# Shift and scale of the first layer loaded in pairs, its first projection begun between them, and a second mixer's adaLN as matmuls

## Chip, cores and metric

One core of one Trainium2 chip. The metric is the device time of the kernel in microseconds (us); the median of the runs is compared. Everything below is one launch on that core.

## What is computed

A decoder trunk of two layers on x (1 x 512 x 1024, float32) with a conditioning vector c (1 x 1024). Each layer has a token mixer (layer 0: native sparse attention, NSA; layer 1: HGRN2, a gated linear recurrence) and a mixture of 16 gated-MLP experts (MoE). Each of these four sub-layers takes a shift, a scale and a gate from c:

```python
cond = jax.nn.silu(c)
for layer in range(DEPTH):
    mod = jnp.einsum('bd,sde->sbe', cond, ada_w[layer]) + ada_b[layer][:, None, :]
    ...
    shift, scale, gate = jnp.split(mod[0], 3, axis=-1)
    h = rms_norm(x, norm_g[layer, 0]) * (1.0 + scale[:, None, :]) + shift[:, None, :]
    y = nsa_mixer(h, ...) if layer % N_MIXERS == 0 else hgrn2_mixer(h, ...)
    x = x + gate[:, None, :] * y
    shift, scale, gate = jnp.split(mod[1], 3, axis=-1)
    ...  # the same norm, then hier_moe, then the gated residual
```

Two pieces matter here. `cond @ ada_w` (adaLN) is one row of 1024 numbers times a 1024 x 3072 matrix for each of the four sub-layers. `h @ w_in` is the first thing that a mixer does with the normalized x; in the NSA mixer 512 of its columns are those of the compressed keys and values (called kv here).

## The kernel before, in words

**adaLN.** `ada_parts(l, s)` (L164) gives six parts for sub-layer s of layer l, 512 columns (2 MB of weights) each: t = 0, 1 are the halves of the shift, 2, 3 of the scale, 4, 5 of the gate. Each part is a load and a generator `part(t, w)`. Parts are counted through the program as 6 (2 l + s) + t; below `POOLED` = 16, `part` does 32 matmuls of TensorE (L185) with the conditioning column as the stationary side, eight at a time with a yield after each eight. Numbers 16 to 23, the gate of the second mixer and all of the second MoE, go another way: ACT scales the eight 128 x 512 blocks by their conditioning column (L192), POOL adds the blocks in three steps of 2048, 1024 and 512 columns (L198), and TensorE sums the partitions with four matmuls against ones (L202). Either way the row is copied by DVE (L209), transposed by TensorE (L211) and put into `mod` by DVE (L214, L217); a gate is added into `gg` (L206).

**The start.** SP's queue loads x, then the four adaLN parts of the first sub-layer in the order 0, 2, 1, 3, then the kv weights (`load_cols`, L435), all of them before any matmul. `norm_T` (L258) makes the normalized x and, block by block, transposes it (L275) and applies scale and shift: ACT writes the high part `hThi` (L280), DVE a copy `hf` (L281), and DVE or POOL the low part `hTlo` (L283). With `before`, the blocks of feature rows 0 to 511 (k = 0 to 3) come first, after parts 0, 2 and 1 and a small table (L456); those of rows 512 to 1023 come after part 3.

**The projections.** A float32 product is made of three matmuls: weights and h are each split into a high and a low part, and high x high, low x high and high x low are summed (L337 to L339). `split_k` (L306) splits one 128 x 512 block of weights: high on ACT (L310), low on DVE (L311). `proj_stream` (L317) goes over tiles of 512 columns; it asks for the next tile's weights ahead, and splits them between the matmuls of the tile's last piece. The first tile is kv: four pieces of 128 tokens, 8 x 3 matmuls each, 96 in all.

**The ring.** Weights of adaLN and of projections share `ring`, which has two slots of 2 MB (`RING`), and are loaded by SP's queue (some early ones of the HGRN stage by POOL's). A load waits until its slot's last reader is done, and what stands behind it on the queue waits too.

**The HGRN stage.** `merge(heads(), ada, HADA)` (L1026) weaves three things together: the eight heads' recurrence, the projection stream, and the adaLN parts 16 to 23, one at a time (`in_turn(..., 1)`), 0.45 steps of a part for each step of a head. A head's recurrence doubles its blocks level by level: TensorE makes the scores of a level (`lvA_ps` to `lvD_ps`, L1043 to L1073), DVE multiplies Q and K by decays for the next (L1080, L1081) and TensorE waits for these. The instructions are put into one order for each engine when the program is built. The output product of the mixer (L373 to L375) needs all of the heads' outputs and the last two ring slots, and the second MoE follows.

Of the kernel before, what the change touches and what calls it, by code (L numbers as in the profile page):

```python
# [32 lines left out]
POOLED = 16  # L33
ADDED = 1

PARTS = ((0, 1, 2), (3,))
# [26 lines left out]
def kernel(ctx: ExitStack, tc: tile.TileContext, I, out, dbg=None, upto="all"):  # L63
# [100 lines left out]
    def ada_parts(l, s):  # L164
# [16 lines left out]
        def part(t, w):  # L181
            if 6 * (2 * l + s) + t < POOLED:
                ps = mm_ps("ada_ps")
                for q in range(0, NK, 2):
                    side_by_side([lambda k=k, g=g: nc.tensor.matmul(  # L185
                        ps[32 * g:32 * g + 32, 0:128], cond[:, k:k + 1].to_broadcast([128, 32]),
                        w[:, k, 128 * g:128 * g + 128], start=(k == 0), stop=(k == NK - 1))
                        for k in (q, q + 1) for g in range(4)])
                    yield
            else:  # L190
                for k in range(NK):
                    nc.scalar.activation(w[:, k], w[:, k], AF.Copy, scale=cond[:, k:k + 1])  # L192
                    if k % 2:
                        yield
                n = NK
                while n > ADDED:
                    n //= 2
                    nc.gpsimd.tensor_tensor(w[:, 0:n], w[:, 0:n], w[:, n:2 * n], op=ALU.add)  # L198
                ps = mm_ps("ada_ps")
                for k in range(n):  # L200
                    for g in range(4):
                        nc.tensor.matmul(ps[32 * g:32 * g + 32, 0:128], onef.to_broadcast([128, 32]),  # L202
                                         w[:, k, 128 * g:128 * g + 128], start=(k == 0), stop=(k == n - 1))
                yield
            if t >= 4:
                nc.vector.tensor_add(gg[:, t - 4], gg[:, t - 4], ps[:, 0:128])  # L206
                return
            row = small.tile([128, 128], F32, tag="adarow", bufs=2, name="adarow")
            nc.vector.tensor_copy(row, ps[:, 0:128])  # L209
            tp = tp_ps("ada_tp")  # L210
            nc.tensor.transpose(tp[:, 0:128], row, ident)  # L211
            b0 = (2 * l + s) * 24 + 4 * t
            m4 = mod[:, 4 * t:4 * t + 4]
            nc.vector.tensor_add(m4, tp[:, 0:128:32], cols[:, b0:b0 + 4])  # L214
            if t >= 2:
                g0 = 96 + (2 * l + s) * 8 + 4 * (t - 2)
                nc.vector.scalar_tensor_tensor(m4, m4, 1.0, cols[:, g0:g0 + 4], op0=ALU.add, op1=ALU.mult)  # L217
# [40 lines left out]
    def norm_T(pool, work, mod, load, before=None):  # L258
# [9 lines left out]
        for i, (half, k) in enumerate(blocks):  # L268
            if before and i % 4 == 0:
                before(i // 4)  # L270
# [46 lines left out]
    def proj_stream(pool, h, tiles, ws=None, last=None):  # L317
# [10 lines left out]
        for n, (_, pieces) in enumerate(tiles):  # L328
            nxt = []
            w = tiles[n + 1][0]() if n + 1 < len(tiles) else None  # L330
            for p, (kind, i, done) in enumerate(pieces):
                c = slice(128 * i, 128 * i + 128)
                ps = mm_ps("pr_ps")
                for k in range(NK):
                    a, b = ws[k]
                    if kind == "tok":
                        nc.tensor.matmul(ps, hi[:, k, c], a, start=(k == 0), stop=False)  # L337
                        nc.tensor.matmul(ps, hi[:, k, c], b, start=False, stop=False)  # L338
                        nc.tensor.matmul(ps, lo[:, k, c], a, start=False, stop=(k == NK - 1))  # L339
                    else:  # L340
                        nc.tensor.matmul(ps, a[:, c], hi[:, k], start=(k == 0), stop=False)
                        nc.tensor.matmul(ps, b[:, c], hi[:, k], start=False, stop=False)
                        nc.tensor.matmul(ps, a[:, c], lo[:, k], start=False, stop=(k == NK - 1))
                    if w is not None and p == len(pieces) - 1:
                        nxt.append(split_k(pool, w, k))
                    if k % 2 and k < NK - 1:
                        yield
# [75 lines left out]
    def nsa_heads(l, load, win, m, st, ada0, fill):  # L423
# [6 lines left out]

        def load_cols(c0, step, n):
# [9 lines left out]
        with sb("first") as wk, sb("adaw", bufs=2) as aw:  # L441
            ada0 = [ada0[i] for i in (0, 2, 1, 3)]
            xs = {t: load(wk, t) for t in range(NT)}
            early = [ada0[i][0](p) for i, p in enumerate((ring, aw, aw, ring))]
# [14 lines left out]

            def before(q):  # L460
# [7 lines left out]
            wkvc = []  # L468
            h = norm_T(pool, wk, mods[l, 0], lambda work, t: xs[t], before)
            ws0 = [split_k(wsp, wkvc[0], k) for k in range(NK)]  # L470
# [174 lines left out]
        for half in range(2):  # L645
            with sb("qkv") as qp:
# [3 lines left out]
                with sb("proj") as wk:  # L650
                    if half == 0:
                        with sb("cmp") as cp:
# [3 lines left out]
                                                      for t in range(NT)])] + half_tiles(0, qkv, wk), ws0, last)  # L656
# [18 lines left out]
                            for _ in range(16):  # L675
                                next(s)
# [1090 lines left out]
```

## Time and profile before

| what | value |
| --- | --- |
| runs | median 1475.61 us of 3 (1474.67 to 1477.06) |
| profiled execution | 1478.35 us, its span 1476.5 us |
| mean granted TensorE clock of the span | 0.944 |
| busy: PE, DVE, ACT, POOL | 87%, 49%, 32%, 15% of the span |
| start, until the kv product ends | about 66.8 us |
| HGRN stage, until the second MoE's router | about 850 to 1114 us |

Shares of the span are means over stages with different limits: the rows further below are taken stage by stage. PE is the matmul side of TensorE, PEld its loading of weights, SPq, ACTq and POOLq are queues in which an engine issues loads. A row's "[3.22 <-DVE K L1081]" says that the engine stood idle for 3.22 us before it and that DVE's write of K at line 1081 released it. "PEclk" is the TensorE clock that was granted, as a share of full speed.

### The profile page before, as it was taken

To read this page: it belongs to the slowest core of one execution; us is meant where nothing else is said; L and a number is where in the kernel's file an instruction comes from. 1 tells how busy PE (TensorE), PEld (TensorE's weight loads), DVE (VectorE), ACT (ScalarE), POOL (GpSimd) and SP (SyncE) were. 2 spreads that over 40 slices of the span, in tenths; PEclk is the share of its full clock that TensorE was granted. 3 is DMA by queue.
4 is the path that set the end of the run, shared out by engine and by line. 5 is a ranking of instruction groups with operands and counts; after the bars stand their busy time and mean duration, and the time that the engine had idled before them with its cause. 6 is when DMAs were issued, how large, how long until landed. Compare 5 with 4: busy or idle time off the path is not lost. (4 is left out here: it accounts for less than half of the span.)

```text
span 1476.5 us, 25266 instructions
## 1 busy us (share of the span) xinstructions
PE 1291.1 (87%) x10122; PEld 767.6 (52%) x10123; DVE 723.1 (49%) x1791; ACT 468.1 (32%) x1071; POOL 225.5 (15%) x198
## 2 busy tenths in 40 slices
PE   4998899988989699999983998888979699999983
PEld 3776555765558333333323866566767543333330
DVE  2636886468854722222217476777665641222213
ACT  2523555336533211111115434344533121111110
POOL 1202212222100100000014025222130100000002
PEclk9999999999999799999996999999989799999997
DMA  9702552634564899999986222433338699999995
GB/s 354 206 11 85 176 185 91 252 121 152 192 265 157 282 368 343 376 381 334 384 325 182 86 103 87 157 115 115 115 115 299 235 343 365 360 377 335 367 397 193
DMA packets 168733, 346.42 MB, mean 235 GB/s; under 512 B 17236, under 2 KB 40620, under 8 KB 168605
## 3 DMA queue, kind: packets, MB, share of 16 engines
q1 hardware_dynamic: 135984, 276.80, 52.6%
q0 software_dynamic: 10560, 38.54, 8.0%
q10 hardware_dynamic: 22060, 29.34, 6.0%
q8 instruction: 84, 1.38, 0.4%
q14 instruction: 45, 0.36, 0.1%
HBM read 320.73 MB, written 23.93 MB: 233 GB/s over the span
## 5 line engine op out<-in xcount | busy, mean ns | idle before, releaser
L1452 PE MATMUL h_ps<-w,hgt 128*32 128x256 f32 (+1 forms) x2240 | 332.9, 488 | 0.0
L1452 PEld LDWEIGHTS h_ps<-w,hgt 128*32 128x32 f32 (+1 forms) x2240 | 111.8, 123 | 203.1 <-issue 172.4
L1479 PE MATMUL y_ps<-w,gT 128*32 128x256 f32 (+1 forms) x1120 | 163.6, 499 | 2.5 <-ACT gT L1468 2.1
L1458 DVE TENSOR_TENSOR g<-h_ps,g 32x256 f32<-32x256 f32 (+1 forms) x70 | 38.9, 556 | 253.7 <-ACT g L1456 253.1
L1456 ACT ACTIVATE g<-h_ps 64x512 f32<-64x512 f32 (+1 forms) x52 | 26.8, 516 | 368.2 <-PE h_ps L1452 346.2
L337 PE MATMUL pr_ps<-whi,hThi 128*128 128x512 f32 x288 | 119.6, 417 | 1.8 <-DVE qn L498 1.8
L338 PE MATMUL pr_ps<-wlo,hThi 128*128 128x512 f32 x288 | 115.6, 401 | 0.3 <-DVE wlo L311 0.3
L339 PE MATMUL pr_ps<-whi,hTlo 128*128 128x512 f32 x288 | 115.7, 402 | 0.2 <-DVE hTlo L283 0.2
L1479 PEld LDWEIGHTS y_ps<-w,gT 128*32 128x32 f32 (+1 forms) x1120 | 54.9, 125 | 97.3 <-issue 81.3
L1482 DVE TENSOR_TENSOR y<-y_ps,gate 128x512 f32<-128x512 f32 (+1 forms) x52 | 31.1, 598 | 123.3 <-PE y_ps L1479 107.5
L311 DVE TENSOR_TENSOR wlo<-w,whi 128x512 fp32r<-128x512 f32 x120 | 79.7, 702 | 23.0 <-ACT whi L310 22.8
L310 ACT ACTIVATE whi<-w 128x512 fp32r<-128x512 f32 x120 | 70.8, 629 | 39.0 <-SPq L1589 14.2
L782 ACT ACTIVATE P<-P,nm 128x128 f32<-128x128 f32 (+3 forms) x128 | 70.9, 556 | 36.9 <-DVE nm L780 35.8
L1416 POOL DMA_INDIRECT hg<-xnd,gidxp x26 | 23.7, 913 | 384.8 <-PE hg_tp L1428 383.0
L776 PE MATMUL s_ps<-kT,qT 128*128 128x256 f32 (+3 forms) x256 | 64.8, 358 | 12.0 <-DVE qn L498 6.9
L198 POOL TENSOR_TENSOR w<-w 128x2048 f32<-128x2048 f32 (+2 forms) x24 | 67.0, 2792 | 47.3 <-ACT w L192 46.1
L780 DVE CUSTOM_DVE_ANT_0 P<-s_ps,tb 128x128 f32<-128x128 f32 (+3 forms) x128 | 59.5, 485 | 21.5 <-PE s_ps L776 18.8
L1436 DVE TENSOR_SCALAR hgt<-hg_tp,mod 128x96 f32<-128x96 f32 (+2 forms) x128 | 43.7, 365 | 41.9 <-PE hg_tp L1428 36.4
L337 PEld LDWEIGHTS pr_ps<-whi,hThi 128*128 128x128 f32 x288 | 55.6, 193 | 15.1 <-issue 3.3
L339 PEld LDWEIGHTS pr_ps<-whi,hTlo 128*128 128x128 f32 x288 | 55.4, 192 | 12.2 <-DVE hTlo L283 0.4
L338 PEld LDWEIGHTS pr_ps<-wlo,hThi 128*128 128x128 f32 x288 | 55.9, 194 | 11.0 <-DVE wlo L311 0.7
L821 PE MATMUL p_tp<-ident,P 128*128 128x128 f32 x320 | 52.8, 282 | 8.2 <-DVE P L796 7.9
(361 smaller groups left out, 2121.9 us busy)
## 6 DMA issues: line engine op xcount, KB each, us to landing
w<-in_moe_w_dram SPq DMA_DIRECT2D x120, 1024.0 KB, 9.7
w<-in_moe_w_dram SPq DMA_DIRECT2D x32, 2048.0 KB, 9.5
w<-in_ada_w_dram SPq DMA_DIRECT2D x22, 2048.0 KB, 9.3
w<-in_hgrn_w_in_dram SPq DMA_DIRECT2D x12, 1024.0 KB, 6.9
tb<-tabd ACTq DMA_DIRECT2D x16, 456.0 KB, 3.8
yd<-y ACTq DMA_DIRECT2D x56, 128.0 KB, 5.0
w<-in_nsa_w_in_dram SPq DMA_DIRECT2D x3, 2048.0 KB, 8.1
yd<-zero POOLq DMA_DIRECT2D x12, 512.0 KB, 9.6
```

The costliest lines, as they stand in the source:

```text
L198: nc.gpsimd.tensor_tensor(w[:, 0:n], w[:, 0:n], w[:, n:2 * n], op=ALU.add)
L310: nc.scalar.activation(a, w[:, k], AF.Copy)
L311: nc.vector.tensor_sub(b, w[:, k], a.bitcast(F32))
L337: nc.tensor.matmul(ps, hi[:, k, c], a, start=(k == 0), stop=False)
L338: nc.tensor.matmul(ps, hi[:, k, c], b, start=False, stop=False)
L339: nc.tensor.matmul(ps, lo[:, k, c], a, start=False, stop=(k == NK - 1))
L776: nc.tensor.matmul(sp[:, :n], qT[:, (hd + j) % 8, 128 * t:128 * t + 128], kT[:, v, br, gl, :n], start=(v == 0), stop=(v == 1))
L780: nc.vector.tensor_tensor_reduce(ps, sp[:, :n], tbs[hd + j][:, 384 - 128 * t:512], scale=-1.0, scalar=3.0e38, op0=ALU.add, op1=ALU.min, ac ...
L782: nc.scalar.activation(ps, ps, AF.Exp, bias=nm[:, i:i + 1], scale=-1.0, accum_out=z[:, i:i + 1])
L821: nc.tensor.transpose(tp[:, 128 * (t - kc):128 * (t - kc) + 128], Ps[j][:, offs[t] + 128 * kc:offs[t] + 128 * kc + 128], ident)
L1452: nc.tensor.matmul(ps[m * j:m * j + m, :w], hgt[:, k, r:r + m], ws[half][:, x + i, c:c + w], start=(k == 0), stop=(k == NK - 1))
L1479: nc.tensor.matmul(ps[m * j:m * j + m, :w], gT[:, f, r:r + m], w2v[:, f, w * j:w * j + w], start=(f == 0), stop=(f == 3))
```

## The change

Two edits. First, at the start, the kv weights come as two loads of 1 MB (rows 0 to 511 and 512 to 1023), each behind one pair of adaLN parts (0, 2 and 1, 3); the kv product's first half (k = 0 to 3 of all four token pieces, 48 of 96 matmuls) is done as soon as the norm's first half is there, with part 1 after two pieces, part 3 after four and then the table; `proj_stream` goes on with k = 4 to 7 in the four sums already begun. Second, `part` has only the matmul way: parts 16 to 23 lose their ACT and POOL instructions and have 32 matmuls instead of four.

```diff
-POOLED = 16
-ADDED = 1
-
-PARTS = ((0, 1, 2), (3,))
...
         def part(t, w):
-            if 6 * (2 * l + s) + t < POOLED:
-                ps = mm_ps("ada_ps")
-                for q in range(0, NK, 2):
-                    side_by_side([...])
-                    yield
-            else:
-                for k in range(NK):
-                    nc.scalar.activation(w[:, k], w[:, k], AF.Copy, scale=cond[:, k:k + 1])
-                    if k % 2:
-                        yield
-                n = NK
-                while n > ADDED:
-                    n //= 2
-                    nc.gpsimd.tensor_tensor(w[:, 0:n], w[:, 0:n], w[:, n:2 * n], op=ALU.add)
-                ...
+            ps = mm_ps("ada_ps")
+            for q in range(0, NK, 2):
+                side_by_side([lambda k=k, g=g: nc.tensor.matmul(
+                    ps[32 * g:32 * g + 32, 0:128], cond[:, k:k + 1].to_broadcast([128, 32]),
+                    w[:, k, 128 * g:128 * g + 128], start=(k == 0), stop=(k == NK - 1))
+                    for k in (q, q + 1) for g in range(4)])
                 yield
...
+            if behind and n % 4 == 3:
+                behind(n // 4, (hi, lo))
...
-    def proj_stream(pool, h, tiles, ws=None, last=None):
+    def proj_stream(pool, h, tiles, ws=None, last=None, begun=()):
...
-                ps = mm_ps("pr_ps")
-                for k in range(NK):
+                early = n == 0 and p < len(begun)
+                ps = begun[p] if early else mm_ps("pr_ps")
+                for k in range(4 if early else 0, NK):
...
-            early = [ada0[i][0](p) for i, p in enumerate((ring, aw, aw, ring))]
+            early = []
+            for i, p in enumerate((ring, aw, aw, ring)):
+                early.append(ada0[i][0](p))
+                if i == 1:
+                    wkv = ring.tile([128, 8, 512], F32, tag="w", name="w")
+                if i % 2:
+                    load_rows(wkv, 1024, 2 * i - 2)
...
+            def behind(q, h):
+
+                for k in range(4 * q, 4 * q + 4):
+                    ws0.append(split_k(wsp, wkv, k))
                 if q == 0:
-                    wkvc.append(load_cols(1024, 512, 512))
-                for i in PARTS[q]:
-                    run(ada0[i][1](early[i]))
-                    if i == 2:
-                        table()
...
+                    for t in range(NT):
+                        begun.append(acc_ps("kv_ps") if t < 2 else mm_ps("kv_ps"))
+                        for k in range(4):
+                            tok_product(begun[t], h, ws0[k], t, k)
+                        if t % 2:
+                            run(ada0[2 + t // 2][1](early[2 + t // 2]))
+                    table()
```

In the changed file L181 stands for L185, L192 for L211, L256 for L275, L261 for L280, L293 for L310, L304 to L306 for L337 to L339, L331 to L333 for L341 to L343, and lines behind 600 are ten higher. The order of the attention and of both MoE stages is the same in both programs. It moves at these places.

On SP's queue at the start (x, adaLN weights, kv weights, constants), before:

```order
L1682 DMA xs<-in_x_dram 128x1024 x4
L91 DMA w<-in_ada_w_dram 128x8x512 x4
L435 DMA w<-in_nsa_w_in_dram 128x8x512
L474 DMA cst<-in_shape_consts_dram 128x396
L475 DMA trif<-in_shape_consts_dram 128x128
```

and with the change:

```order
L1692 DMA xs<-in_x_dram 128x1024 x4
L88 DMA w<-in_ada_w_dram 128x8x512 x2
L423 DMA w<-in_nsa_w_in_dram 128x4x512
L88 DMA w<-in_ada_w_dram 128x8x512 x2
L423 DMA w<-in_nsa_w_in_dram 128x4x512
L484 DMA cst<-in_shape_consts_dram 128x396
```

The first half of the kv weights has moved ahead of two adaLN parts; the bytes are the same.

On ACT at the end of the first norm (`hThi` is the norm's output, `whi` the high part of split weights; `w_192` of before is kv, `w_520` of before and `w_573` of the change the next tile), before:

```order
L310 ACTIVATE whi_467<-w_192 128x512
L280 ACTIVATE hThi_165<-h_tp_403,mod00_106 128x256
L280 ACTIVATE hThi_165<-h_tp_414,mod00_106 128x256
L280 ACTIVATE hThi_165<-h_tp_425,mod00_106 128x256
L310 ACTIVATE whi_471<-w_192 128x512
L310 ACTIVATE whi_475<-w_192 128x512
L280 ACTIVATE hThi_165<-h_tp_436,mod00_106 128x256
```

and with the change:

```order
L261 ACTIVATE hThi_168<-h_tp_472,mod00_106 128x256
L459 DMA tabd_134<-tabs_461 16x1040
L261 ACTIVATE hThi_168<-h_tp_472,mod00_106 128x256
L261 ACTIVATE hThi_168<-h_tp_483,mod00_106 128x256
L261 ACTIVATE hThi_168<-h_tp_494,mod00_106 128x256
L261 ACTIVATE hThi_168<-h_tp_483,mod00_106 128x256
L261 ACTIVATE hThi_168<-h_tp_505,mod00_106 128x256
L293 ACTIVATE whi_620<-w_573 128x512
L261 ACTIVATE hThi_168<-h_tp_494,mod00_106 128x256
L293 ACTIVATE whi_624<-w_573 128x512
L261 ACTIVATE hThi_168<-h_tp_505,mod00_106 128x256
```

The splits of kv have moved ahead of these rows, the table's store in among them, and two splits of the next tile stand ahead of the norm's last two activations (one row on the gate weights between them is left out).

On PE in the HGRN stage, around one adaLN part (`pr_ps` is the projection stream, `ho_ps` and `lvA_ps` the recurrence), before:

```order
L1124 MATMUL ho_ps<-vS,AD 128x128
L1124 MATMUL ho_ps<-vS,AO 128x128 x3
L1124 MATMUL ho_ps<-vS,AD 128x128
L202 MATMUL ada_ps<-w,onef 32x128 x4
L337 MATMUL pr_ps<-whi,hThi 128x512
L338 MATMUL pr_ps<-wlo,hThi 128x512
L339 MATMUL pr_ps<-whi,hTlo 128x512
```

and with the change:

```order
L332 MATMUL pr_ps<-hThi,wlo 128x512
L333 MATMUL pr_ps<-hTlo,whi 128x512
L1053 MATMUL lvA_ps<-Q,K 32x32 x16
L181 MATMUL ada_ps<-w,cond 32x128 x16
L304 MATMUL pr_ps<-whi,hThi 128x512
L305 MATMUL pr_ps<-wlo,hThi 128x512
L306 MATMUL pr_ps<-whi,hTlo 128x512
```

A part's matmuls, four in one place before, are 32 in up to four places, and they are now the first readers of the load. At the end of the stage the last adaLN part stood between the last head's levels, with `out_ps` behind it; now its last eight matmuls are ahead of the last head's levels and the first `out_ps` matmuls stand among the levels.

## Rows read from the trace of the kernel before

**Rows 1.** The page's first lines: the span, and each engine's busy us, share of the span and instructions.

```profile
span 1476.5 us, 25266 instructions
PE 1291.1 (87%) x10122; PEld 767.6 (52%) x10123; DVE 723.1 (49%) x1791; ACT 468.1 (32%) x1071; POOL 225.5 (15%) x198
```

**Rows 2.** Busy time in stretches of the start. Columns: stretch (us), its length, busy us (and instructions) of PE, PEld, DVE, ACT and POOL, granted clock, DMA share, GB/s.

```profile
33.00:47.43 14.43, 11.33 (x112) 8.97 (x109) 11.93 (x24) 10.71 (x22) 3.01 (x2) 0.88 1.02 226
47.43:66.80 19.37, 19.09 (x86) 15.26 (x84) 10.88 (x20) 8.65 (x15) 4.95 (x2) 1.00 0.72 207
66.80:110.50 43.70, 43.67 (x328) 30.59 (x327) 13.74 (x34) 9.02 (x22) 3.04 (x3) 1.00 0.14 49
```

**Rows 3.** PE in the order of time at the start (start, us, operation): the first adaLN part with the cause of the wait ahead, the fourth, and two kv matmuls.

```profile
15.40 3.64 PE L185 MATMUL ada_ps<-w,cond 128*32 128x128 f32 x64 [7.03 <-DMA w<-in_ada_w_dram]
...
34.85 1.95 PE L185 MATMUL ada_ps<-w,cond 128*32 128x128 f32 x64
...
45.44 0.39 PE L338 MATMUL pr_ps<-wlo,hThi 128*128 128x512 f32 x1
45.67 0.39 PE L339 MATMUL pr_ps<-whi,hTlo 128*128 128x512 f32 x1
```

**Rows 4.** ACT and its queue at the start, in the order of time: the table's store, the first split of the kv weights, a row of the norm.

```profile
33.88 2.28 ACTq L458 DMA_DIRECT2D tabd<-tabs  x1
...
39.81 1.15 ACT L310 ACTIVATE whi<-w 128x512 fp32r<-128x512 f32 x2
...
42.86 1.69 ACT L280 ACTIVATE hThi<-h_tp,mod 128x256 fp32r<-128x256 f32 x3
```

**Rows 5.** SP's queue at the start: the next tile's loads (four) and the one behind.

```profile
43.44 10.54 SPq L435 DMA_DIRECT2D w<-in_nsa_w_in_dram  x5
```

**Rows 6.** Busy time in the HGRN stage, from just ahead of the first part with POOL additions to the end of the projection stream's matmuls, and from there to the output product. Columns as in rows 2.

```profile
850.00:1080.36 230.36, 204.17 (x2303) 155.76 (x2302) 162.38 (x310) 98.51 (x190) 71.64 (x31) 0.94 0.33 111
1080.36:1098.29 17.93, 9.62 (x262) 7.83 (x261) 14.24 (x29) 5.49 (x12) 4.14 (x3) 0.75 0.60 218
```

**Rows 7.** Busy time in the seven stretches of that stage in which POOL adds (L198); the last of them, and the sum of all seven. Columns as in rows 2.

```profile
1066.56:1083.47 16.91, 15.65 (x134) 12.73 (x132) 3.15 (x5) 7.39 (x15) 16.59 (x6) 1.00 0.00 1
sum 68.21, PE 44.67 PEld 33.10 DVE 47.78 ACT 13.40 POOL 66.93; mean PE 6.38 PEld 4.73 DVE 6.83 ACT 1.91 POOL 9.56
```

**Rows 8.** The same for the eight stretches between them, from 850 to 1088 us: the sum.

```profile
sum 169.79, PE 164.68 PEld 127.06 DVE 119.69 ACT 86.37 POOL 7.77; mean PE 20.58 PEld 15.88 DVE 14.96 ACT 10.80 POOL 0.97
```

**Rows 9.** One of those stretches in the order of time, all engines.

```profile
1025.78 8.45 POOL L198 TENSOR_TENSOR w<-w 128x2048 f32<-128x2048 f32 x3 [7.74 <-ACT w L192]
...
1025.88 4.76 DVE L1081 TENSOR_TENSOR K<-K,Tc 128x256 f32<-128x256 f32 x1
...
1026.85 0.39 PE L342 MATMUL pr_ps<-hThi,wlo 128*128 128x512 f32 x1
...
1030.70 0.68 PE L1063 MATMUL lvC_ps<-Q,K 128*64 128x64 f32 x8 [3.22 <-DVE K L1081]
...
1032.00 0.63 PE L342 MATMUL pr_ps<-hThi,wlo 128*128 128x512 f32 x1
```

**Rows 10.** Another of them, in the order of time.

```profile
950.62 8.72 POOL L198 TENSOR_TENSOR w<-w 128x2048 f32<-128x2048 f32 x3
...
951.49 4.25 DVE L1138 TENSOR_TENSOR on<-on,gS 128x512 f32<-128x512 f32 x1
...
959.67 0.66 PE L1043 MATMUL lvB_ps<-Q,K 128*32 128x32 f32 x32 [6.17 <-DVE K L1081]
```

**Rows 11.** The instructions of three lines: duration in ns (least, median, most), first and last start in us, forms.

```profile
L198 POOL TENSOR_TENSOR w<-w x24: 1288/2415/4770, 862.9 to 1082.1; 128x2048 f32<-128x2048 f32 x8, 128x1024 f32<-128x1024 f32 x8, 128x512 f32<-128x512 f32 x8
...
L192 ACT ACTIVATE w<-w,cond x64: 705/712/727, 857.8 to 1072.0; 128x512 f32<-128x512 f32 x64
...
L1081 DVE TENSOR_TENSOR K<-K,Tc x56: 409/418/4759, 852.9 to 1097.5; 128x256 f32<-128x256 f32 x56
```

**Rows 12.** PE in the order of time: a quarter of an adaLN part as matmuls, during the attention, and the row behind it; then the four matmuls of a part in the HGRN stage, and the row behind them. A record of a matmul in a column group counts twice (x16 for eight, x8 for four).

```profile
388.16 0.64 PE L185 MATMUL ada_ps<-w,cond 128*32 128x128 f32 x16
388.73 0.44 PE L821 MATMUL p_tp<-ident,P 128*128 128x128 f32 x2
...
949.49 0.45 PE L202 MATMUL ada_ps<-w,onef 128*32 128x128 f32 x8
...
949.87 0.50 PE L341 MATMUL pr_ps<-hThi,whi 128*128 128x512 f32 x1
```

**Rows 13.** Loads of adaLN weights in the HGRN stage, by SP's queue and by POOL's: KB each, us from issue to landing.

```profile
w<-in_ada_w_dram SPq DMA_DIRECT2D x1, 2048.0 KB, 8.1
...
w<-in_ada_w_dram POOLq DMA_DIRECT2D x1, 2048.0 KB, 8.4
```

**Rows 14.** The end of the HGRN stage in the order of time: the last adaLN part's matmuls, the load of the output weights, their split, the first output matmul.

```profile
1085.99 0.66 PE L202 MATMUL ada_ps<-w,onef 128*32 128x128 f32 x16
1086.59 0.99 SPq L91 DMA_DIRECT2D w<-in_hgrn_w_out_dram  x2
...
1097.52 2.55 ACT L313 ACTIVATE whi<-w,gain 128x512 fp32r<-128x512 f32 x4
...
1098.29 0.79 PE L373 MATMUL out_ps<-whi,ohi 128*128 128x512 f32 x1 [1.34 <-ACT whi L313]
```

**Rows 15.** The second MoE. Columns as in rows 2.

```profile
1120.00:1450.00 330.00, 308.19 (x2124) 138.05 (x2124) 101.71 (x296) 62.24 (x132) 22.57 (x26) 0.96 0.94 338
```

More of the change, by code (lines that the diff above doesn't have):

```diff
@@ L256, in rms_rows, with norm_T @@
         return rs
-    def norm_T(pool, work, mod, load, before=None):
+    def norm_T(pool, work, mod, load, before=None, behind=None):
         hi = pool.tile([128, NK, T], F32R, name="hThi")
@@ L267, in norm_T @@
             blocks = [(half, k) for q in (0, 4) for half in range(2) for k in (q, q + 2)]
-        for i, (half, k) in enumerate(blocks):
-            if before and i % 4 == 0:
-                before(i // 4)
+        for n, (half, k) in enumerate(blocks):
+            if before and n % 4 == 0:
+                before(n // 4)
             c = slice(256 * half, 256 * half + 256)
@@ L315, in split_k, with tok_product @@
         return a, b
-    def proj_stream(pool, h, tiles, ws=None, last=None):
+    def tok_product(ps, h, ws, i, k):
+        hi, lo = h
+        a, b = ws
+        c = slice(128 * i, 128 * i + 128)
+        nc.tensor.matmul(ps, hi[:, k, c], a, start=(k == 0), stop=False)
+        nc.tensor.matmul(ps, hi[:, k, c], b, start=False, stop=False)
+        nc.tensor.matmul(ps, lo[:, k, c], a, start=False, stop=(k == NK - 1))
+    def proj_stream(pool, h, tiles, ws=None, last=None, begun=()):
         hi, lo = h
@@ L429, in nsa_heads, with load_rows @@
         tabd = dram.tile([HEADS, TBL], F32, name="tabd")
+        def load_rows(w, c0, k0):
+            loads.append(nc.sync.dma_start(out=w[:, k0:k0 + 4], in_=win[128 * k0:128 * k0 + 512, c0:c0 + 512]
+                                           .rearrange("(k p) n -> p k n", p=128)))
         def load_cols(c0, step, n):
@@ L458, in table @@
                 nc.scalar.dma_start(out=tabd, in_=tabs)
+            ws0, begun = [], []
             def before(q):
-                if q == 0:
-                    wkvc.append(load_cols(1024, 512, 512))
-                for i in PARTS[q]:
-                    run(ada0[i][1](early[i]))
-                    if i == 2:
-                        table()
-            wkvc = []
-            h = norm_T(pool, wk, mods[l, 0], lambda work, t: xs[t], before)
-            ws0 = [split_k(wsp, wkvc[0], k) for k in range(NK)]
+                for i in (0, 1) if q == 0 else ():
+                    run(ada0[i][1](early[i]))
+            def behind(q, h):
+                for k in range(4 * q, 4 * q + 4):
+                    ws0.append(split_k(wsp, wkv, k))
+                if q == 0:
+                    for t in range(NT):
[5 more added lines that the diff above has]
+                    table()
+            h = norm_T(pool, wk, mods[l, 0], lambda work, t: xs[t], before, behind)
             trif = wk.tile([128, 128], F32, name="trif")
@@ L655, in nsa_heads @@
                                                      [("tok", t, lambda ps, t=t: nc.scalar.activation(kv[:, t], ps, AF.Copy) and None)
-                                                      for t in range(NT)])] + half_tiles(0, qkv, wk), ws0, last)
+                                                      for t in range(NT)])] + half_tiles(0, qkv, wk), ws0, last, begun)
                             w1 = cp.tile([128, 2, 16, DH], F32, name="cw1")
@@ L674, in nsa_heads @@
                             nc.gpsimd.memset(x2[:, :, 0:4, 256:264], 0.0)
-                            for _ in range(16):
+                            for _ in range(8):
                                 next(s)
```

16 lines of the change are left out of this document (3 added, 13 removed).

## Prediction

> **What bounds the kernel now.** I first take each engine's share of the span: TensorE is busy for 87%, no other engine for half [rows 1]. That is a mean, so I then cut the span into stretches and look in each for time in which TensorE stands idle or runs at a lower clock. Only the start and the HGRN stage are edited. The stages behind them have their old order. The attention follows the start with TensorE gapless, 43.67 of 43.70 us [rows 2], and the second MoE is fed by loads, DMA share 0.94 [rows 15]. So what the start or the HGRN stage gives should move everything behind it and not be eaten.
>
> In the start, TensorE is busy in 11.33 of 14.43 us just before the kv product runs freely and then in 19.09 of 19.37 [rows 2]: almost all of the 96 kv matmuls stand behind the norm, while earlier TensorE waits for loads (7.03 us before the first part [rows 3]).
>
> The HGRN stage is the large case. From 850 to 1080.36 us TensorE is busy for 204.17 of 230.36, at a clock of 0.94: 26.2 us idle [rows 6]. The seven stretches in which POOL adds adaLN weights hold 68.21 us, and TensorE is busy in 44.67: 23.5 us idle in under a third of the time [rows 7]. The eight stretches between them hold 169.79 us with 164.68 busy: 5.1 idle [rows 8]. The order of time says how POOL does this. An addition starts at 1025.78, DVE's product for K starts 0.1 us later and takes 4.76 us, and TensorE stands for 3.22 us until K is written [rows 9]; the middle of that line's 56 is 418 ns [rows 11]. At 951.49 the same happens to another product with two SBUF operands (4.25 us), and a level's matmuls wait 6.17 us [rows 10]. Then the clock follows: a projection matmul takes 0.39 us before the wait and 0.63 after [rows 9].
>
> **The change, part by part.** The sum goes against the profiled execution, 1478.35 us with its span of 1476.5; that stands 2.74 above the median, 1475.61, and I subtract this at the end.
>
> *Price of the added matmuls.* A quarter of a part as matmuls starts at 388.16 and the next work at 388.73: 0.57 us, so 2.28 a part. The four matmuls against ones took from 949.49 to 949.87: 0.38 [rows 12]. Eight parts cost 8 x (2.28 - 0.38) = **+15.2 us** on TensorE. That is on the path: these matmuls fill no gap of their own, and I count all of it. A cold clock would make it more: the first part took 3.64 and the fourth 1.95 us [rows 3], so the ends are 8 x 1.57 = 12.6 and 8 x 3.26 = 26.1.
>
> *The removed work.* POOL loses 24 additions, all but a few of its 66.93 us in the seven stretches [rows 7], ACT 64 scalings of 0.71 us, 45 us [rows 11]. Neither engine is the bound, so this is worth only what waits for it: 23.5 us of idle time in the seven stretches, of which 16.91 - 15.65 = 1.3 lies in the last one, at the end of the stage [rows 7]. I take **-22.3** for 850 to 1080; 26.2 - 22.3 = 3.9 us of idle time stays. What stays is the levels' own chain, at 418 ns a product.
>
> *Clock.* 204.17 us at 0.94 is a loss of at most 204.17 x 0.06 = 12.2 us [rows 6]. The falls come behind the waits [rows 9], but the added matmuls and load waits can make new ones; between 0 and -12.2 I take **-8**.
>
> *New waits.* Before, ACT was the first reader of an adaLN load, with POOL and a part's yields behind it; now TensorE is, in order, with the projection and the levels queued behind. A load takes 8.1 us from issue to landing [rows 13], and its slot comes free when a tile's last block is split, by the order some 28 to 40 projection matmuls of 0.23 us [rows 3], 6 to 9 us, ahead of the part. So some of eight loads are late by 1 to 2 us. Nothing in the rows shows this wait. Its ends are 0 and 8 x 8.1 = 65 us (no overlap at all); it is nearest to the lower one, since all but two or three of the loads are issued a whole part ahead: **+2**. On the other side, the ring's projection weights no longer stand behind POOL's chain; I count nothing for that, as TensorE never waited for one there.
>
> *End of the stage.* Between the stream's last matmul and the output product TensorE is busy in 9.62 of 17.93 us [rows 6]. DVE starts there with K held up by the last addition, the last adaLN part's matmuls sit between the levels, and only behind them is the load of the output weights issued, at 1086.59; their split starts at 1097.52 and the first output matmul at 1098.29 [rows 14]. By the new order that slot is free before the last head's levels, and output matmuls stand among them. The ends are 0 (the levels' chain sets the end as before) and 8.3 (all of the idle time); I take the middle, **-4**.
>
> *Start.* 48 kv matmuls at 0.23 us [rows 3] are 11.0 us that could lie beside loads: one end is -11. The other end is +1: the norm's rows and the splits share ACT and DVE, which were busy for 10.71 and 11.93 of 14.43 us [rows 2], the table's store, 2.28 us of ACT's queue [rows 4], now falls between the norm's halves, and TensorE does the second norm half's transposes only after the first 48 matmuls, the two parts and the table. Four loads of 2 MB lie between the first part at 15.40 and kv's split at 39.81 [rows 3, 4], so at most 6.1 us each; by that the second load is there at about 21 and the first norm half, with half a load behind it, at about 26, the 48 matmuls are spread by the splits to about 43, part 3 ends at about 45 and the norm's second half at about 50: that is 48 matmuls less behind the norm, but the norm ends some 3 us later, and two splits of the next tile stand ahead of its last two rows on ACT. Those wait for a load that was issued at 43.44 and took its turn of 10.54 us [rows 5]. So the last kv matmul comes at about 63 instead of 66.5: **-3.5**.
>
> Sum: 15.2 - 22.3 - 8 + 2 - 4 - 3.5 = -20.6; 1478.35 - 20.6 = 1457.7, and less the 2.74, **1455.0 us** against the median.
>
> A rule that speaks against this. Row first: TensorE is the busiest engine, 87%, and POOL the least busy, 15% [rows 1]. The Trainium skill, "Perfetto Trace Analysis", section Identifying the Most-Contended Engine, says to optimise the engine of highest occupancy first, and to judge TensorE by how long it loads weights rather than by matmul time. By that the kernel should get slower where the busiest engine takes over work from idle ones, which is rival 3; the stage's own rows decide against it, since the 26.2 us stand idle there.
>
> **Rivals.**
>
> 1. *The waits come back as others.* The levels' chain on DVE or the adaLN loads hold TensorE in the places where POOL did; two thirds of the 22.3 us (15) stay. For it: the clock at 0.94 also outside the additions and 5.1 us idle there [rows 8]. Against: the products stretch only while POOL adds [rows 9, 10]. Time: 1455 + 15 = 1470. Chance 0.13.
> 2. *The start gives nothing.* ACT stands at the next tile's splits, and the norm's last rows with it, until the load lands. TensorE runs out of kv matmuls and the 3.5 us go: 1458.5, or 1462 if it costs as much. Chance 0.14.
> 3. *Slower: TensorE is the bound and its idle time was not POOL's.* If the levels and not the additions set those waits, 15.2 us are added and nothing leaves but the start's: 1475.6 + 15.2 - 3.5 = 1487. Against it are the seven stretches. Chance 0.03.
> 4. *Slower: TensorE stands at its own loads.* The ring has two slots, and eight loads are now waited for in TensorE's order. Without my +2 the gain is 22.6, so it decides from 22.6 / 8 = 2.8 us for each load; at 4 us, half of a landing [rows 13], it is 32, and the time 1475.6 - 22.6 + 32 = 1485. For it: load and slot times are of one size. Against: other parts lie between issue and use. Chance 0.05.
> 5. *The change doesn't do what it says.* The order has the 32 matmuls for each part and no additions, and the kv matmuls ahead of the second norm half. Chance 0.01.
>
> **How the numbers follow.** My forecast has 0.64, rivals 1 to 5 have 0.13, 0.14, 0.03, 0.05 and 0.01. About 0.2%, 3 us, is what a measurement tells from no change here. Faster is the forecast, rival 2 and most of rival 1: 0.87; within 0.2% is the worst of rival 1, rival 5 and the mildest of rival 4: 0.05; slower is the rest, 0.08. The low end takes the clock's whole 12.2, 6 for the end of the stage and 8 for the start: 4.2 + 2 + 4.5 = 10.7 below 1455, **1444**; the ends do not all come at once. The high end takes rival 2, and rival 1 with it almost whole: **1472**. What is left out is rivals 3 to 5 and the edges of the others, less than 0.2.
>
> **What would show it.** In the changed profile: no DVE product of L1091 (L1081 of before) above 1 us; the 850 to 1080 stretch shorter by some 13 us, with TensorE idle for less than 8 us and a clock above 0.95; eight parts at 2.2 to 2.6 us of TensorE's time; waits of TensorE on adaLN loads of 2 us in all; the first output matmul within 14 us of the stream's end; the last kv matmul at about 63 us and the next rows of the attention as much earlier. I am wrong if waits named for adaLN loads exceed 10 us, if the levels still wait for K as long, or if the kv product ends no earlier than 66 us.

## The result, and the profile after

The changed kernel takes 1453.84 us (median of 4 runs, 1452.09 to 1459.31) against 1475.7 for the kernel before: a ratio of 0.9858, interval 0.9828 to 0.9887, so 21.9 us less where 20.6 were forecast. A second series gave 1455.06 (6 runs) with the same ratio, 0.9858 (0.9832 to 0.9884).

The page of the changed kernel, as [rows 1]:

```profile
span 1457.5 us, 26079 instructions
PE 1293.2 (89%) x10570; PEld 768.4 (53%) x10571; DVE 690.7 (47%) x1791; ACT 429.6 (29%) x1007; POOL 156.1 (11%) x174
```

POOL lost 69 us of work, ACT 38 and DVE 32, with as many DVE instructions as before: the same products ran shorter. TensorE has 448 more records, which are 8 x 28 = 224 more matmuls in column groups, and only 2 us more busy time over the span, in part since it ran at a better clock (0.955 against 0.944).

The HGRN stage in the stretches that answer to [rows 6] (850 to 1080.36 there is 846 to 1064.6 here, and the second row is as long a stretch behind it; columns as there):

```profile
846.00:1064.60 218.60, 212.36 (x2815) 162.30 (x2814) 132.01 (x313) 60.23 (x126) 7.21 (x8) 0.98 0.38 127
...
1064.60:1082.50 17.90, 12.52 (x208) 10.13 (x208) 14.80 (x31) 9.40 (x16) 1.38 (x1) 0.71 0.47 165
```

230.36 us became 218.60. TensorE is idle for 6.2 us instead of 26.2, and its clock is 0.98 instead of 0.94. DVE's product for K, as in [rows 11]:

```profile
L1091 DVE TENSOR_TENSOR K<-K,Tc x56: 410/418/423, 848.9 to 1080.1; 128x256 f32<-128x256 f32 x56
```

Its longest was 4759 ns and is now 423. What TensorE waited for in the 218.60 us (in all, times, longest):

```profile
PE ada_ps L181 <- DMA w<-in_ada_w_dram: 2.2, 3, 1.0
PE lvB_ps L1053 <- DVE ss L1142: 1.5, 1, 1.5
PE pr_ps L304 <- DVE on L1147: 0.9, 1, 0.9
PE lvB_ps L1053 <- DVE K L1091: 0.6, 2, 0.3
```

The first row is the new wait that the prediction priced at 2 us. The end of the stage, as [rows 14]:

```profile
1064.64 0.64 PE L181 MATMUL ada_ps<-w,cond 128*32 128x128 f32 x16
...
1074.27 0.64 PE L1067 MATMUL lvB_ps<-Q,K 128*32 128x32 f32 x16 [2.26 <-DVE K L1091]
...
1077.66 0.80 PE L364 MATMUL out_ps<-whi,ohi 128*128 128x512 f32 x1 [0.62 <-ACT ohi L358]
```

The first output matmul comes 13 us behind the stream, not 18, but the last head's levels still wait for DVE, now at its usual pace: a chain without other work beside it. How much of this the kernel keeps shows at the second MoE's first router matmul, before and with the change:

```profile
1144.72 1.07 PE L1225 MATMUL lg_ps<-wra,xt 128*128 128x20 f32 x8
...
1125.89 1.07 PE L1235 MATMUL lg_ps<-wra,xt 128*128 128x20 f32 x8
```

It comes 64.3 us behind the stream before and 61.2 us with the change.

The start did not go as forecast. TensorE in the second half of kv:

```profile
51.08 0.39 PE L306 MATMUL kv_ps<-whi,hTlo 128*128 128x512 f32 x1
55.84 0.80 PE L306 MATMUL kv_ps<-whi,hTlo 128*128 128x512 f32 x1 [4.37 <-POOL hTlo L264]
56.44 0.63 PE L304 MATMUL kv_ps<-whi,hThi 128*128 128x512 f32 x1
```

and ACT with its queue at that time:

```profile
44.80 0.60 ACTq L680 DMA_DIRECT2D wg<-in_nsa_w_in_dram  x1
...
52.89 0.52 ACT L628 ACTIVATE wghi<-wg 128x384 fp32r<-128x384 f32 x1 [4.15 <-DMA wg<-in_nsa_w_in_dram]
53.32 1.00 ACT L261 ACTIVATE hThi<-h_tp,mod 128x256 fp32r<-128x256 f32 x2
```

The split of the small gate weights (`wghi`) stands ahead of four of the norm's last rows on ACT, and their load was issued at 44.80, two microseconds after SP had begun to issue the next tile's 2 MB. ACT, then POOL, then TensorE wait, and TensorE comes back at half clock (granted clock 0.50 from 55.84 to 60 us, 0.63 instead of 0.39 us a matmul). In this execution the kv product ends at 66.2 us, 0.6 earlier than before, and at the attention's last matmuls (417.4 against 417.2) nothing of that is left. In the eight traces with this start and this order of ACT it ends at 63.2 to 66.2, and the wait at POOL's `hTlo` is 0.3 to 4.5 us.

One part of the difference between the two profiled executions isn't the change's. Between 422 and 440 us both run the attention's output product and what follows it, in the same order (the faster one gets further):

```profile
422.00:440.00 18.00, 16.23 (x65) 12.64 (x64) 8.67 (x15) 4.22 (x10) 0.00 (x0) 0.81 0.95 371
```

is the kernel before, and the changed one has

```profile
422.00:440.00 18.00, 15.27 (x71) 11.39 (x70) 11.53 (x19) 4.94 (x10) 0.00 (x0) 1.00 0.97 379
```

The clock fell in one and not in the other. From the attention's end to the HGRN stage the trace of before took 430.9 us, all 13 later ones 423.9 to 428.4, the changed one 426.7. So about 4 of the 19 us between the two profiled spans come from a stretch that no edit touched. Single executions differ by some us in this way; the medians below carry the verdicts, the traces the mechanisms.

### The profile page after: what moved, and what is told of

Same layout as the page of the kernel before. It is cut to its first block, busy times and chain, and to the rows that moved or that the text cites. A ratio compares the mean times of both kernels' runs of the same rounds, so it can differ in the third digit from the quotient of the medians.

```text
span 1457.5 us, 26079 instructions
## 1 busy us (share of the span) xinstructions
PE 1293.2 (89%) x10570; PEld 768.4 (53%) x10571; DVE 690.7 (47%) x1791; ACT 429.6 (29%) x1007; POOL 156.1 (11%) x174
## 3 DMA queue, kind: packets, MB, share of 16 engines
q8 instruction: 88, 1.44, 0.4%
## 5 line engine op out<-in xcount | busy, mean ns | idle before, releaser
L304 PE MATMUL pr_ps<-whi,hThi 128*128 128x512 f32 x256 | 107.1, 419 | 2.9 <-DVE qn L508 1.8
L306 PE MATMUL pr_ps<-whi,hTlo 128*128 128x512 f32 x256 | 102.0, 399 | 0.3 <-DVE hTlo L264 0.3
L305 PE MATMUL pr_ps<-wlo,hThi 128*128 128x512 f32 x256 | 102.1, 399 | 0.0
L293 ACT ACTIVATE whi<-w 128x512 fp32r<-128x512 f32 x120 | 72.0, 630 | 64.2 <-SPq L1599 15.3
L786 PE MATMUL s_ps<-kT,qT 128*128 128x256 f32 (+3 forms) x256 | 65.3, 360 | 11.5 <-DVE qn L508 6.9
L181 PE MATMUL ada_ps<-w,cond 128*32 128x128 f32 x1536 | 62.1, 291 | 11.1 <-DMA w<-in_ada_w_dram 10.5
L790 DVE CUSTOM_DVE_ANT_0 P<-s_ps,tb 128x128 f32<-128x128 f32 (+3 forms) x128 | 59.5, 486 | 21.9 <-PE s_ps L786 18.3
L1444 ACT ACTIVATE hgt<-hg_tp,mod 128x96 f32<-128x96 f32 (+2 forms) x128 | 48.3, 421 | 35.9 <-DVE hgt L1446 32.2
L304 PEld LDWEIGHTS pr_ps<-whi,hThi 128*128 128x128 f32 x256 | 49.2, 192 | 17.2 <-issue 5.1
L786 PEld LDWEIGHTS s_ps<-kT,qT 128*128 128x128 f32 x256 | 40.7, 195 | 33.0 <-issue 16.2
```

What stands on the lines that cost most here:

```text
L181: side_by_side([lambda k=k, g=g: nc.tensor.matmul(ps[32 * g:32 * g + 32, 0:128], cond[:, k:k + 1].to_broadcast([128, 32]), w[:, k, 128 * g ...
L293: nc.scalar.activation(a, w[:, k], AF.Copy)
L786: nc.tensor.matmul(sp[:, :n], qT[:, (hd + j) % 8, 128 * t:128 * t + 128], kT[:, v, br, gl, :n], start=(v == 0), stop=(v == 1))
L790: nc.vector.tensor_tensor_reduce(ps, sp[:, :n], tbs[hd + j][:, 384 - 128 * t:512], scale=-1.0, scalar=3.0e38, op0=ALU.add, op1=ALU.min, ac ...
```

## The experiments

"Stage" is the time from the heads' first matmul to the last of the projection stream, in the kernel's trace; "rest" is from there to the end of the span.

| kernel | median us | ratio to before (interval) | stage | rest |
| --- | --- | --- | --- | --- |
| before | 1475.2 to 1475.7 | 1 | 232.2 | 396.2 |
| the change, first and second series | 1453.84, 1455.06 | 0.9858, 0.9858 | 220.5, 218.9 | 392.9, 393.4 |
| adaLN edit alone | 1461.06 | 0.9906 (0.9892 to 0.9920) | 219.6 | 391.8 |
| start edit alone | 1470.32 | 0.9968 (0.9956 to 0.9979) | 233.8 | 395.5 |
| before without POOL additions | 1446.12 | 0.9797 (0.9779 to 0.9815) | 206.8 | 393.3 |
| change with idle additions | 1479.22 | 1.0024 (1.0009 to 1.0039) | 245.3 | 392.4 |
| change with idle memsets | 1454.84 | 0.9856 (0.9826 to 0.9886) | 221.8 | 393.0 |
| change, gate weights first | 1450.23 | 0.9849 (0.9818 to 0.9881) | 220.0 | 391.7 |
| change, parts in one piece | 1446.45 | 0.9808 (0.9782 to 0.9833) | 205.9 | 395.5 |
| change, matmuls twice | 1469.73 | 0.9963 (0.9948 to 0.9978) | 229.3 | 392.0 |
| change, five steps a part | 1444.98 | 0.9806 (0.9783 to 0.9828) | 209.2 | 392.4 |
| one piece and gate weights first | 1438.36 | 0.9751 (0.9729 to 0.9774) | 205.5 | 391.9 |
| no additions, both start edits | 1440.45 | 0.9756 (0.9730 to 0.9781) | 206.6 | 391.1 |

**1. The adaLN edit alone**, in the kernel before.

```diff
-POOLED = 16
+POOLED = 24
```

> The kernel before with the second edit alone: parts 16 to 23 as 32 matmuls each, the start as it was. Theory (POOL's additions held DVE up, TensorE waited for DVE): the terms of the prediction without the start, 15.2 - 22.3 - 8 + 2 - 4 = -17, so some 17 us below before; in the changed kernel's trace the stage and its end gave about 11.8 + 3.2 = 15. Rival (TensorE is the bound, the gain came from the start): 15 us above before.

Measured: 14.2 us below before (interval 11.8 to 15.9), and the stage of the changed kernel. TensorE's added matmuls were more than paid for, but the 17 us of the sum lie outside the interval: its adaLN terms were some 3 us too good.

**2. The start edit alone** (the changed kernel with the old `part`).

> The kernel with the change, but parts 16 to 23 by ACT and POOL as before: the first edit alone. The prediction's term: 3.5 us below before. From the changed kernel's trace, where ACT stood 4.15 us for the load of the gate weights ahead of the norm's last rows and the kv product ended only 0.6 us earlier: 0 to 1 us below before. Rival (the start gave what the stage did not): 5 us or more below before.

Measured: 4.9 us below before (interval 3.1 to 6.5), so the 0 to 1 us that I read from the changed kernel's one trace were wrong. 14.2 and 4.9 make 19.1, the change 20.4 to 21.9: within the intervals the edits add up.

**3. Without POOL's additions**, in the kernel before.

```diff
-ADDED = 1
+ADDED = 8
```

> The kernel before with POOL's additions alone taken out: ACT scales the eight blocks as before, and TensorE sums all eight with 32 matmuls against ones. Theory (the additions are what slows DVE): nearly the gain of the adaLN edit, 12 to 18 us below before, with DVE's K product at 0.42 us throughout. Rival (it was ACT's scaling, or ACT as the first reader of the loads, that held the stage): no gain, or up to 15 us above before for the added matmuls.

Measured: 29.1 us below before, more than theory or rival allowed. ACT's scaling does no harm, and the additions were the cause of at least the gain that I had counted; but this kernel, with the old start, beats the changed one by 8 us. That gain had no place in my account, and experiments 7 and 10 look for it.

**4. Idle additions, and 5. idle memsets.** The changed kernel, with this at the head of `part` for parts 16 to 23 (the scratch `z` is 1024 columns):

```diff
+                nc.gpsimd.tensor_tensor(z, z, w[:, 0:2], op=ALU.add)
+                for n in (2, 2, 1):
+                    nc.gpsimd.tensor_tensor(z[:, 0:n], z[:, 0:n], z[:, 2 - n:2], op=ALU.add)
```

and for the memsets one addition of a single column and `nc.gpsimd.memset(z[:, 0:n], 0.0)` for n in (2, 2, 2, 1).

> The kernel with the change, and for each of parts 16 to 23 four POOL additions on a scratch buffer (three of 1024 columns, one of 512; the first also reads the part's load, so that they run when it has landed). Nothing waits for their sums; the order of the other engines is unchanged. Theory (POOL's additions slow DVE's products that read two SBUF operands, whoever needs the sum): DVE's K products stretch to 1.5 us and more again, TensorE waits for K, and the time rises by 10 to 25 us above the changed kernel. Rival (what cost the time was that parts waited for POOL's sum): the time of the changed kernel within 3 us.

> As the kernel with idle additions, but POOL only writes: for each of parts 16 to 23 one addition of a single column that reads the part's load, and then four memsets of the scratch buffer (three of 1024 columns, one of 512). Theory (it is the second SBUF operand that DVE's product and POOL's addition compete for): DVE's K products stay at 0.42 us and the time within 3 us of the changed kernel, 1454, some 25 below the kernel with idle additions. Rival (any long POOL work at that place holds DVE, or the heads' POOL operations that stand behind it): 10 us or more above the changed kernel.

The stage with the idle additions (columns as in [rows 6]), then DVE's K product and TensorE's two largest waits there, in a view each:

```profile
840.30:1085.60 245.30, 221.78 (x2857) 168.23 (x2857) 168.57 (x316) 61.11 (x129) 70.57 (x40) 0.95 0.33 113
```

```profile
L1100 DVE TENSOR_TENSOR K<-K,Tc x56: 410/419/2576, 845.1 to 1101.1; 128x256 f32<-128x256 f32 x56
```

```profile
PE lvB_ps L1062 <- DVE K L1100: 7.1, 4, 3.5
PE lvA_ps L1062 <- DVE K L1100: 4.5, 2, 3.1
```

and with the idle memsets the stage and the K product:

```profile
843.50:1065.30 221.80, 214.18 (x2853) 163.70 (x2852) 135.42 (x316) 61.43 (x129) 37.62 (x48) 0.98 0.37 125
```

```profile
L1100 DVE TENSOR_TENSOR K<-K,Tc x56: 405/418/430, 848.4 to 1080.8; 128x256 f32<-128x256 f32 x56
```

The order of instructions is the same in both, and nobody needs what POOL writes. Additions add 33 us to DVE's 316 instructions and 24 us to the time; memsets add 1.5 us to DVE and nothing that shows to the time, though POOL is busy for 30 us more than without them (the additions made it 63). So the cost of before was not that a part waited for POOL's sum. It was that DVE's products ran longer while POOL added. The Trainium skill, "SBUF — State Buffer", section Who interferes with whom, says that a DVE instruction with two SBUF inputs contends with a GpSimd instruction that reads SBUF and not with one that only writes: both traces agree, K's product at up to 2576 ns beside the one and at most 430 beside the other.

**6. Gate weights first.** The load is moved ahead of the four loads of the compression's weights (`cw1`, `cw2`).

```diff
+                            wg = cp.tile([128, 8, 48], F32, name="wg")
+                            nc.scalar.dma_start(out=wg, in_=win[:, 2560:2608].rearrange("(k p) n -> p k n", p=128))
                             w1 = cp.tile([128, 2, 16, DH], F32, name="cw1")
```

> The kernel with the change, with the load of the gate weights issued first on ACT's queue, ahead of the four loads of the compression's weights. Theory (at the start ACT stood 4.15 us for that load, ahead of the norm's last rows, and TensorE 4.37 us behind it): 2 to 6 us below the changed kernel, the kv product ending by 63 us. Rival (ACT's next row, a split of the next tile, waits for a load that lands at the same time): 0 to 1 us below the changed kernel.

ACT in its trace:

```profile
43.41 0.52 ACT L628 ACTIVATE wghi<-wg 128x384 fp32r<-128x384 f32 x1 [1.46 <-DMA qg<-in_nsa_q_gain_dram]
47.64 0.57 ACT L261 ACTIVATE hThi<-h_tp,mod 128x256 fp32r<-128x256 f32 x1 [3.71 <-PE h_tp L256]
```

The split is done at 44 instead of 53, TensorE no longer waits for POOL's `hTlo`, and kv ends at 61.7 us. By the medians of the series this is 4.8 us, by the ratios it can't be told from the change: that the wait leaves is shown, its price isn't. Beside the edit of experiment 7 the same move is worth 8 us (0.9808 to 0.9751, intervals apart), but the traces don't give that to the start. With the gate weights first, DVE's order changes too: a product that needs the query gain `qg` now stands ahead of the last adaLN row. In experiment 11's trace, DVE and then TensorE:

```profile
45.39 0.36 DVE L496 SCALAR_TENSOR_TENSOR gkq<-gkq,qg 128x192 f32<-128x192 f32 x1 [4.91 <-DMA qg<-in_nsa_q_gain_dram]
45.67 0.28 DVE L194 COPY adarow<-ada_ps 128x128 f32<-128x128 f32 x1
...
46.01 0.33 PE L196 MATMUL ada_tp<-ident,adarow 128*128 128x128 f32 x1 [3.24 <-DVE adarow L194]
```

TensorE waits there for 1.1 us in the trace of this experiment, 3.2 and 3.4 in those of 11 and 12, and in these two the kv product ends at 64.3 and 65.3 us, no earlier than without the move. Between the traces of 7 and 11 there are 6.2 us: 0.3 up to the end of kv, 1.9 from there to the heads, 0.4 in the stage and 3.5 behind it, all of these behind the second MoE's first router matmul, where neither edit reaches. Where the 8 us come from stays open.

**7. Parts in one piece** (for parts 16 to 23).

```diff
+            late = 6 * (2 * l + s) + t >= 16
+            for _ in range(4 if late else 0):
+                yield
             ps = mm_ps("ada_ps")
-            for q in range(0, NK, 2):
+            step = NK if late else 2
+            for q in range(0, NK, step):
...
-                    for k in (q, q + 1) for g in range(4)])
+                    for k in range(q, q + step) for g in range(4)])
```

> The kernel with the change, but parts 16 to 23 take four empty steps and then do their 32 matmuls in one piece, as the kernel before did its four: the same matmuls, the same conditioning column, no ACT, no POOL. In the kernel without POOL additions such a piece took 1.91 us where four quarters take 2.3, TensorE's waits were 3 us instead of 6, and the last two parts fell into the gaps behind the stream. Theory (the quarters and their place cost the difference): 8 to 16 us below the changed kernel. Rival (ACT's scaling ahead of the matmuls did it, by taking the wait for the load off TensorE): within 3 us of the changed kernel.

Measured: 7.4 to 8.6 us below the change. The stage of its trace, 205.9 us, is about that of experiment 3 (206.8), so ACT's scaling had no share in the shorter stage. By the medians experiment 3 lies 14.9 us below experiment 1, its pair with the old start; what that is more than 8.6 isn't explained. Two things were altered here, the quarters and the number of steps.

**8. The change again.**

> The changed kernel once more, as the reference of this series: 1454 us within 3. If the kv product's end at 66.2 us in its first trace was that execution's clock and not the order, it now ends nearer to 64 us, as in the two other traces with the first edit (64.2 and 64.4).

1455.06 us, and the kv product ends at 63.2; TensorE waits 1.0 us for POOL's `hTlo` where the first trace had 4.4.

**9. The matmuls twice** (`half` is half of `cond`).

```diff
-                    ps[32 * g:32 * g + 32, 0:128], cond[:, k:k + 1].to_broadcast([128, 32]),
-                    ... for k in (q, q + 1) for g in range(4)])
+                    ps[32 * g:32 * g + 32, 0:128], (half if n == 2 else cond)[:, k:k + 1].to_broadcast([128, 32]),
+                    ... for r in range(n) for k in (q, q + 1) for g in range(4)])
```

> The kernel with the change, and each of the 32 matmuls of parts 16 to 23 done twice, with half of the conditioning column each time, so that the sums stay the same: 64 matmuls a part. Theory (the added matmuls lie on TensorE's path): 8 parts by 2.3 us, 15 to 20 us above the changed kernel's 1454. Rival (they lie in time in which TensorE would wait anyway, and the price of 15.2 us in the sum was never paid): less than 6 us above it.

Measured: 15 to 16 us above the change; the stage of its one trace is 9 to 10 longer, with TensorE's clock at 1.00 there. They are on the path, at less than the price of the sum, whose 2.28 us a part would make 18.2. In the stages of the traces, the time in which TensorE does these matmuls and nothing else is 27.7 us here and 14.7 and 14.3 in the two of the change: 13 more.

**10. Five steps a part**, quarters kept.

```diff
+            if 6 * (2 * l + s) + t >= 16:
+                yield
             ps = mm_ps("ada_ps")
```

> The kernel with the change and one empty step ahead of each of parts 16 to 23, so that a part takes five steps as it did before the change and the last part and a half come behind the projection stream; the matmuls stay in quarters. Theory (the place of the last parts, in the gaps of the last head, is what the kernel in one piece won by): 3 to 5 us below the changed kernel. Rival (it is the quarters themselves, 8 x 0.5 us, and TensorE's waits for loads): within 2 us of the changed kernel.

Measured: 9 to 10 us below the change, as much as the one piece. The place was worth something, as the theory said, but its size was half of what was measured; the quarters cost nothing that the medians show. The end of the stage in this trace:

```profile
1047.96 0.64 PE L183 MATMUL ada_ps<-w,cond 128*32 128x128 f32 x16
...
1051.94 1.10 PE L183 MATMUL ada_ps<-w,cond 128*32 128x128 f32 x32
...
1053.29 1.54 PE L183 MATMUL ada_ps<-w,cond 128*32 128x128 f32 x48
...
1055.39 0.62 PE L183 MATMUL ada_ps<-w,cond 128*32 128x128 f32 x16
```

and the stage before it, in the view of stretches and of TensorE's waits:

```profile
838.10:1047.30 209.20, 207.00 (x2677) 158.06 (x2676) 133.21 (x313) 60.31 (x129) 8.25 (x8) 1.00 0.37 122
```

```profile
PE lvB_ps L1055 <- DVE K L1093: 1.0, 3, 0.3
PE ada_ps L183 <- DMA w<-in_ada_w_dram: 0.8, 1, 0.8
```

Two parts now stand among the last head's levels, where the changed kernel stood idle for K. They aren't free there: the second MoE's first router matmul comes 62.8 us behind the stream, where it was 61.2. "Rest" doesn't show this (392.4 against 392.9 and 393.4), since from that matmul to the end of the span the traces differ by 4 us (328.9 to 332.7) without an edit. Against the second trace of the change, whose clock in the stage is 1.00 too, the stage is 9.7 us shorter: TensorE is busy for 4.7 us less, 3.8 of it by the two parts, and idle for 2.2 instead of 7.2. Its waits for loads fell from 2.9 us to 0.8, and one wait each for DVE's `ss` (1.5) and `on` (0.9) are gone; those for K are as they were. That they fell because the parts come later is argued, not shown.

**11 and 12. Put together**: the diffs of 6 and 7; and the diffs of 3 and 6 on the kernel of experiment 2.

> The two edits that helped, together: the gate weights' load first at the start, and parts 16 to 23 in one piece after four empty steps. If they add up: 8.6 + 4.8 = 13 us below the changed kernel, about 1441. If the start's gain is lost later: 1446.

> The same with ACT's scaling kept, as in the kernel without POOL additions: ACT scales each block when it has landed and TensorE sums all with 32 matmuls against ones, with the start's edit and the gate weights' load first. That kernel was at 1446.1 without any edit of the start. If the start's edits add up (4.9 + 4.8): about 1437. If ACT's scaling gives nothing over the pieces with the conditioning column: within 2 us of the kernel with the two edits.

1438.36 and 1440.45 us. The first is 37 us below before and 15 to 17 below the change, a little more than expected, though by its trace not through an earlier end of kv (experiment 6). In the second the start's edits gave 5.7 us on experiment 3 where 9.7 were expected. Keeping ACT's scaling makes no difference that can be told: the two intervals overlap almost wholly.

## Why the prediction was right, step by step

- *The bound.* Right. TensorE's idle time in the stage was POOL's doing: rival 3 falls with experiments 1, 3, 4 and 5.
- *Price of the matmuls, +15.2.* On the path, as said, and somewhat too large: by the same working, doubling them adds 8 x 2.28 = 18.2, and it cost 15 to 16. A part took TensorE about 1.9 us, less than the 2.2 to 2.6 that I had named as a sign.
- *Idle time and new waits, -22.3 + 2.* Right: 26.2 us became 6.2, so -20.0, and the waits on loads are 2.2 us in all. Rivals 1 and 4 asked for 10 and more.
- *Clock, -8.* Right, as an estimate: by the working of the prediction 212.36 x 0.02 = 4.2 of the 12.2 us are left, so 8 came back. Busy time says 7.0, since it rose by 8.2 where 15.2 were to be added, and less if the matmuls cost less. In the second trace the clock in the stage is 1.00. The stretch took 11.8 us less, against a forecast of 13.1.
- *End of the stage, -4.* A little less: the second MoE's router comes 3.1 us closer to the stream in both traces of the change, and "rest" became 2.8 to 3.3 us shorter. The middle of its bounds was luck: what was left there is the levels' chain.
- *Start, -3.5.* The size is within experiment 2's interval (4.9; 3.1 to 6.5), the working isn't. I named the next tile's splits as what would hold the norm's last rows, and had left the row of the gate weights between them out. That row is what ACT stood at (4.15 us), and with its load first this wait is gone while the splits stay where they were. Rival 2 had the right place and the wrong load. (Nor does a load of the next tile take the 10.54 us of [rows 5], which span five issues: the four landed 7.3 us after theirs.) And one sign that I had named for being wrong came true in the changed profile: the kv product ended at 66.2 us, not before 66. The second trace has 63.2, as forecast, so for the start single traces decide nothing, and where its 4.9 us are gained isn't shown.
- *The sum.* 20.6 forecast, 20.4 to 21.9 measured: nearer than its terms deserve. The adaLN terms (17.1 against 14.2 alone) were too good and the start (3.5 against 4.9) too small, and the two edits together gave 1 to 3 us more than the two alone, which is within the noise. That the profiled pair fits as well is luck too: it has 0.6 us from the start and about 4 from a stretch without edits.
- *What the sum did not see.* I counted all of the 15.2 us because the matmuls "fill no gap of their own". That holds for the order as it is, and hid the larger lever: with four steps instead of five the parts run out before the gaps of the last head. One empty step a part is worth 9 to 10 us.

## What to carry to other kernels

Cut a span into the stretches in which one suspect runs and those in which it doesn't, and compare the bound engine's idle time in both: that found 23.5 of 28.6 us in under a third of the stage, and made a change pay that adds work to the busiest engine. When work moves to the bound engine, look where its pieces land: the last two parts cost TensorE 3.8 us within the stream, and in the gaps behind it they put the next stage off by 1.6. And read every row that stands on an in-order engine ahead of the one you follow; a load of 128 x 8 x 48 numbers, issued behind 2 MB on another queue, held ACT for up to 4.3 us, and moving it put another small load in the way. When a trace shows the wait leave, look whether the stage behind it comes earlier as well.

## What the runs showed of the hardware

Additions of POOL that nobody waits for cost the kernel 24 us through DVE: 33 us of longer DVE instructions for 63 us of POOL work. Memsets, 30 us of them, cost no time that shows. A short stall cost twice here: behind 4.37 us of waiting the next kv matmuls took 0.63 instead of 0.39 us, at a granted clock of 0.50. But a wait doesn't decide it alone: in the attention's output product TensorE waited 1.44 us for DVE in both profiled executions, and behind it the matmuls took 0.63 us in the one (clock 0.81 over those 18 us) and 0.40 in the other (1.00). That may be why runs of one kernel spread over 3 to 11 us here; no run shows it.
